# A decoder block on one core: more block products in the MLP, weight sums of the down projection formed in DRAM, another order of the background work

## The chip, the cores and the metric

The kernel runs on one core of one Trainium2 chip. The metric is device time of one execution in microseconds (us), lower is better. Engines are named as in the profile: PE is TensorE's matmul, PEld its weight load, DVE is VectorE, ACT ScalarE, POOL GpSimd, SP SyncE; "SPq" and "POOLq" in a row are the issuing of a DMA on that engine's queue.

## The reference

One layer on 512 rows of width 1024, all in float32: a sparse attention with three branches, a sliding-window attention, an MLP with a causal convolution of width 3, and a gated side input. What matters here is the MLP:

```python
h = x @ w_in            # and both attentions: queries, keys, gates, ...
x = x + rmsnorm(concat(o_nsa, o_swa) @ w_o, attn_post_g)
h = rmsnorm(x, mlp_pre_g)
a, u = split(h @ w_gate_up, [2816])           # 1024 -> 2 x 2816
a = causal_dwconv(a, conv_w, conv_b)
y = (gelu(a, approximate=True) * u) @ w_down  # 2816 -> 1024
x = x + rmsnorm(y, mlp_post_g)
x = x + (p @ w_ple) * sigmoid(x @ w_ple_gate)
```

## The kernel before

**Products.** Each float32 operand is held as two float32r parts, a high part and the remainder. `mm3` forms a product by three matmuls into one PSUM bank: high by high (L165), low by high (L168), high by low (L169). A weight of 128 x 1024 arrives raw by one DMA on SyncE (`raw`, L154; or L156); ACT copies its high part (L144) and DVE subtracts it to get the low part (L148), both in `weight`. There are three pairs of slots for split weights ("wh"), two for raw ones ("wr"), and others among tags such as "p" and "kn".

**Up stage (`mlp_up`).** The 2816 columns make 22 tiles of 128 columns, each with a gate weight and an up weight; tiles 0 and 1 are done first, from weights that were ready earlier. A plain tile is two gemms of 8 products on 512 columns: 48 matmuls of 512 columns. Up to tile `RAW_LAST` the gemms take the rows before their normalization and the result is scaled by the row factors afterwards: DVE L1161, POOL L1163 in `mlp_tile`. Later tiles take normalized rows (`hn`), which `normalized` makes in small steps between the gemms, with their half sums (`ht`, L1052 to L1062). After that each tile ends in the convolution and the gelu (`conv`, DVE L1146, ACT L1144 and L1147) and is kept as two parts in `y`.

**Blocked tiles.** The tiles in `BLOCKED` use a scheme of seven half-size products in place of eight (`blocked_tile`): 84 matmuls of 256 columns. It needs sums of parts of the weights. These are formed in DRAM: a DMA on SyncE copies a part (`block_copies`, 256 KB each, 28 of them, issued in attention, one at every third call of `fill` after the tenth), then DMAs with addition on POOL's queue add other parts to it (`block_additions`, L1199, 28 of them), three after each gemm of the up stage. `fill` is called between the steps of attention to put filling matmuls, loads and copies there; its DMA is `load_late` (L295). Moves of the queries and keys to the partitions where attention wants them are `move` (L298), also on SyncE.

**Down stage (`mlp_down`).** Eight output tiles of 128 columns; six go as three pairs (`pair_of_tiles`), of whose 22 input tiles the first twelve are done as six block products and the others plainly. For a block product a weight of 256 KB is loaded and DVE forms the three sums with four operations on 128 columns (`block_weight`, L1079 to L1082) before ACT and DVE split it. The half sums of `y` are made by `sums_of` (L1068 and `half_sums`). Each pair uses six PSUM banks, and `block_sums` puts them together.

**What sets the order.** The program text gives each engine its instructions through a scheduler that keeps the order where it is told to (`keep_in_program_order`), and moves the rest. `pin` ties a DMA with addition behind a given matmul. A DMA on SyncE waits on its own queue for the slot that it fills and for the sum that it reads; what stands behind it on SyncE waits too.

Of the kernel before, what the change touches and what calls it, by code (L numbers as in the profile page):

```python
# [76 lines left out]
COPY_FROM, COPY_STEP = 10, 3


class Block:  # L80
# [971 lines left out]
    def half_sums(self, b, t, parts):  # L1052
# [5 lines left out]
        nc.vector.tensor_sub(t[:, 3, :], b[1][0], t[:, 1, :])  # L1058
        for i, o in enumerate(parts):
            v = t[:, 2 * i : 2 * i + 2, :].rearrange("p a n -> p (a n)")  # L1060
            nc.scalar.activation(o[:, 0, :], v, AF.Copy)
            nc.vector.tensor_sub(o[:, 1, :], v, o[:, 0, :].bitcast(F32))  # L1062

    def sums_of(self, i):
# [5 lines left out]
        self.half_sums([[f[:, k, hs] for hs in HALF] for k in range(2)], self.u([P, 4, H], F32, STAG[i]), self.tt[i])  # L1070

    def block_weight(self, c, i, tag):

# [1 line left out]
        r = self.wrp.tile([P, 7 * P], F32, tag="wr", name=self.nm("wr")) if tag == "wr" else self.u([P, 7 * P], F32, tag)
        src = self.io["down"][c : c + 2, :, 2 * i * P : (2 * i + 2) * P].rearrange("c p n -> p c n")
        nc.sync.dma_start(r[:, : 4 * P].rearrange("p (c n) -> p c n", c=2), src)
        b = [r[:, k * P : (k + 1) * P] for k in range(7)]
        nc.vector.tensor_sub(b[4], b[0], b[2])  # L1079
        nc.vector.tensor_add(b[2], b[2], b[3])  # L1080
        nc.vector.tensor_sub(b[5], b[2], b[0])
        nc.vector.tensor_sub(b[6], b[1], b[5])  # L1082
        return self.weight(r, 7 * P, early=True)

    def block_products(self, c, i, wt, banks, last=False):
        d, e, p1, p5, p6, p7 = banks
        y1, y2 = self.y[2 * i], self.y[2 * i + 1]
        ta, tb = self.tt[i]
        a, b = slice(0, H), slice(H, T)
        for ps, k, x in ((p1, 0, y1[:, :, a]), (p6, 5, ta[:, :, b]), (p7, 4, tb[:, :, a]), (p5, 2, ta[:, :, a])):  # L1090
            self.mm3(ps[:, a], wt, k * P, x, i == 0, i == KP - 1)
        for ps, k, x in ((d[:, a], 1, y2[:, :, a]), (d[:, b], 6, y2[:, :, b]), (e[:, a], 3, tb[:, :, b])):
            self.mm3(ps, wt, k * P, x, False, last and k != 1)
# [398 lines left out]
```

## Time and profile before

| | |
|---|---|
| median of 3 runs | 666.39 us (665.5 to 667.02) |
| the profiled execution | 662.78 us |
| its span in the profile | 660.9 us |
| granted TensorE clock | 1.00 |
| up stage, by PE | 252.4 to 489.3 us |
| down stage, by PE | 489.3 to 611.3 us |
| busy: PE, DVE, ACT, POOL | 646.9, 501.9, 361.2, 174.3 us |

Attention lies before 223.3 us, the output projection and the norm between 223.3 and 252.4, the last norm and the gated side input after 611.3. In a row of the timeline the first two numbers are the start and the length in us, then come engine, line, operation, output <- inputs by the program's names; in square brackets stands how long the engine had been idle and what ended it. In a row of the waits the three numbers are the total in us, how often, and the longest. In a row of a window: the stretch, its length, the busy time of PE, PEld, DVE, ACT and POOL with the count of instructions, the granted clock, the DMA engines' busy share and GB/s. In a row of DMA issues the last two numbers are the size of one transfer and the median time from issue to landing in us.

### The profile page before, as it was taken

Reading aid. Unit: us, or ns where it says so; the run is one execution under the profiler, and the core shown is the slowest. Engines: PE = TensorE matmul, PEld = TensorE weight load, DVE = VectorE, ACT = ScalarE, POOL = GpSimd, SP = SyncE. Lnnn points to the kernel's source line nnn. Section 1 sums busy time; section 2 is a strip of 40 time slices with the busy share of each in tenths; the row PEclk is TensorE's granted clock in tenths of the full one; section 3 lists DMA queues with packets and bytes.
Section 4 is the critical chain, followed back from the end, with each engine's and each line's share of the span. In section 5 each row is a group of like instructions: output and inputs, shape, how many; then the busy total and the mean of one; then the engine's idle time right before and its main releaser. Section 6 shows DMA issues by size and latency. Waiting matters only on the chain.

```text
span 660.9 us, 10545 instructions
## 1 busy us (share of the span) xinstructions
PE 646.9 (98%) x3701; PEld 563.3 (85%) x3701; DVE 501.9 (76%) x1048; ACT 361.2 (55%) x667; POOL 174.3 (26%) x260
## 2 busy tenths in 40 slices
PE   9999899999999999999999999999999999999997
PEld 8988678878888888888778889998898898899986
DVE  6895587978756469699998766767699876757873
ACT  7464487978888476445465544554444434334351
POOL 1111488678487163216330000000000010102000
PEclk9999999999999999999999999999999999999999
DMA  8437891321364529929774355343322234287032
GB/s 302 170 108 242 272 339 42 83 55 50 80 187 164 160 95 257 300 81 182 170 229 154 121 165 160 123 131 113 96 75 87 72 113 127 66 293 258 31 112 79
DMA packets 39076, 98.22 MB, mean 149 GB/s; under 512 B 4656, under 2 KB 12848, under 8 KB 37680
## 3 DMA queue, kind: packets, MB, share of 16 engines
q1 hardware_dynamic: 37536, 90.13, 41.7%
q0 software_dynamic: 1344, 7.34, 6.2%
q8 instruction: 29, 0.48, 0.3%
q14 instruction: 23, 0.19, 0.1%
q10 hardware_dynamic: 144, 0.08, 0.1%
HBM read 83.90 MB, written 20.97 MB: 159 GB/s over the span
## 4 chain that ended last, share of the span: by engine, by line
PE 73%; DVE 15%; DMA 5%; ACT 3%; issue 2%; POOL 0%; SPq 0%; ACTq 0%; DVEq 0%
DMA mlpdown_wr<-in_down_dram 3%; PE mlpup_pss L168 3%; PE mlpup_pss L169 3%; PE mlpup_pss L165 3%; DVE mlpdown_wh L148 2%; PE nsa_pso L613 2%; DVE mlpup_s L1146 2%; PE nsa_pst L580 2%; PE mlpup_psmm L168 2%; PE mlpup_psmm L169 2%; PE mlpup_psmm L165 2%; PE mlpup_pst L169 2%; PE mlpup_pst L168 2%; PE mlpup_pst L165 2%; DVE mlpup_wh L148 2%
## 5 line engine op out<-in xcount | busy, mean ns | idle before, releaser
L291 POOL TENSOR_TENSOR mlpdown_s<-mlpdown_s,mlpdown_s 128x512 f32<-128x512 f32 x6 | 8.9, 1478 | 241.3 <-ACT mlpdown_s L290 241.2
L144 ACT ACTIVATE mlpup_wh<-mlpup_wr 128x1024 fp32r<-128x1024 f32 x31 | 32.7, 1056 | 32.8 <-DMA mlpup_wr<-in_gu_dram 8.5
L144 ACT ACTIVATE mlpdown_wh<-mlpdown_wr 128x896 fp32r<-128x896 f32 (+2 forms) x27 | 26.3, 979 | 43.0 <-DMA mlpdown_wr<-in_down_dram 15.5
L148 DVE TENSOR_TENSOR mlpup_wh<-mlpup_wr,mlpup_wh 128x1024 fp32r<-128x1024 f32 x31 | 37.8, 1219 | 9.9 <-PE mlpup_psmm L168 4.7
L603 POOL TENSOR_SCALAR nsa_u<-nsa_u,nsa_nrc,gate 128x512 f32<-128x512 f32 (+3 forms) x64 | 38.6, 615 | 15.0 <-DVE nsa_nrc L739 9.9
L705 ACT ACTIVATE nsa_u<-nsa_u,nsa_nnm 128x512 f32<-128x512 f32 (+3 forms) x64 | 35.4, 554 | 7.2 <-DVE nsa_nnm L698 7.1
L148 DVE TENSOR_TENSOR mlpdown_wh<-mlpdown_wr,mlpdown_wh 128x896 fp32r<-128x896 f32 (+2 forms) x27 | 31.2, 1163 | 9.3 <-ACT mlpdown_wh L144 8.8
L165 PE MATMUL mlpup_pss<-mlpup_u,mlpup_wh 128*128 128x256 f32 (+1 forms) x108 | 34.8, 322 | 0.1
L168 PE MATMUL mlpup_pss<-mlpup_u,mlpup_wh 128*128 128x256 f32 (+1 forms) x108 | 34.8, 322 | 0.0
L169 PE MATMUL mlpup_pss<-mlpup_u,mlpup_wh 128*128 128x256 f32 (+1 forms) x108 | 34.8, 322 | 0.0
L585 DVE TENSOR_TENSOR nsa_u<-nsa_pst,nsa_u 128x512 fp32r<-128x512 f32 (+1 forms) x43 | 29.4, 686 | 6.8 <-ACT nsa_u L582 6.5
L1146 DVE SCALAR_TENSOR_TENSOR mlpup_s<-mlpup_s,cols,mlpup_s 128x511 f32<-128x511 f32 (+1 forms) x30 | 27.3, 913 | 6.2 <-ACT mlpup_s L1144 6.0
L148 POOL TENSOR_TENSOR fill_wh<-fill_wr,fill_wh 128x1024 fp32r<-128x1024 f32 (+2 forms) x13 | 24.5, 1887 | 28.7 <-ACT fill_wh L144 28.7
L698 DVE CUSTOM_DVE_ANT_0 nsa_u<-nsa_pss,biastables_u 128x224 f32<-128x224 f32 (+3 forms) x64 | 27.9, 447 | 5.4 <-PE nsa_pss L639 4.8
L148 DVE TENSOR_TENSOR mlpup_wh<-mlpup_u,mlpup_wh 128x1024 fp32r<-128x1024 f32 x16 | 19.6, 1224 | 14.2 <-ACT mlpup_wh L144 11.2
L582 ACT ACTIVATE nsa_u<-nsa_pst 128x512 fp32r<-128x512 f32 x43 | 25.4, 593 | 8.5 <-PE nsa_pst L580 8.1
L144 ACT ACTIVATE mlpup_wh<-mlpup_u 128x1024 fp32r<-128x1024 f32 x16 | 17.0, 1060 | 22.1 <-PE mlpup_pss L168 11.2
L168 PE MATMUL mlpup_psmm<-mlpup_u,mlpup_wh 128*128 128x256 f32 (+1 forms) x88 | 27.5, 313 | 1.3 <-DVE mlpup_wh L148 1.3
L169 PE MATMUL mlpup_psmm<-mlpup_u,mlpup_wh 128*128 128x256 f32 (+1 forms) x88 | 27.4, 312 | 0.0
L165 PE MATMUL mlpup_psmm<-mlpup_u,mlpup_wh 128*128 128x256 f32 (+1 forms) x88 | 27.4, 311 | 0.0
L613 PE MATMUL nsa_pso<-nsa_u,vnatural_u 128*128 128x512 f32 x72 | 25.8, 423 | 0.4 <-DVE nsa_s L597 0.2
L165 PE MATMUL mlpdown_psmm<-mlpup_u,mlpdown_wh 128*128 128x512 f32 (+1 forms) x76 | 26.0, 344 | 0.0
(535 smaller groups left out, 2372.9 us busy)
## 6 DMA issues: line engine op xcount, KB each, us to landing
mlpup_wr<-in_gu_dram SPq DMA_DIRECT2D x17, 512.0 KB, 3.9
blocks<-in_gs_dram SPq DMA_DIRECT2D x28, 256.0 KB, 5.5
mlpup_u<-in_gu_dram SPq DMA_DIRECT2D x9, 512.0 KB, 4.1
blocks<-in_gs_dram POOLq DMA_DIRECT2D x14, 256.0 KB, 7.2
blocks<-blocks POOLq DMA_DIRECT2D x14, 256.0 KB, 5.0
mlpup_wr<-in_gs_dram SPq DMA_DIRECT2D x7, 512.0 KB, 3.5
mlpup_wr<-blocks SPq DMA_DIRECT2D x7, 512.0 KB, 4.0
mlpup_u<-blocks SPq DMA_DIRECT2D x7, 512.0 KB, 3.7
```

The source lines that it names most:

```text
L144: h = nc.scalar.activation(hi, raw, AF.Copy)
L148: l = eng.tensor_sub(lw, raw, hi.bitcast(F32))
L165: r = self.pin(mm(ps, hi, x[:, 0, :], start=start, stop=False))
L168: mm(ps, lo, x[:, 0, :], start=False, stop=False)
L169: self.last = mm(ps, hi, x[:, 1, :], start=False, stop=stop).ins
L582: nc.scalar.activation(t[:, 0, :], pt, AF.Copy)
L585: nc.vector.tensor_sub(t[rs, part, :], pt[rs], t[rs, 0, :].bitcast(F32))
L603: self.nc.gpsimd.tensor_scalar(ap, ap, col, gate, op0=ALU.mult, op1=ALU.mult)
L613: self.att(nc.tensor.matmul(po, v, t[:, part, :], start=start, stop=stop))
L698: nc.vector.tensor_tensor_reduce(dst, src, dist, op0=ALU.add, op1=ALU.min, scale=SLOPES[8 + 4 * g + r], scalar=start, accum_out=out)
L705: nc.scalar.activation(dst, dst, AF.Exp, bias=nm[:, r, b : b + 1], scale=-1.0, accum_out=sm[:, r, b : b + 1])
L1146: nc.vector.scalar_tensor_tensor(c[:, k:], a[:, : T - k], w(2 - k), c[:, k:], op0=ALU.mult, op1=ALU.add)
```

## The change

- **Blocked tiles.** Eight, tiles 10, 11, 13, 14, 16, 17, 19 and 20, instead of seven (9, 11, 13, 15, 17, 19, 21). `RAW_LAST` goes from 7 to 6.
- **Down.** The host packs the parts of the down weights of the three pairs (`gd`), and their sums are formed in DRAM (`down_sums`) by the same copies and additions as in up, 384 KB each: 12 copies and 12 additions. Two blocks go together as a group with two weights (1024 and 768 columns), each raw weight by two DMAs (L1083 now), and DVE forms no sums of weights any more. A pair uses four PSUM banks instead of six. `ORDER` says where the groups stand among the plain parts.
- **Copies.** 32 of 256 KB in attention, from call 44 on at every fourth; the 12 of 384 KB are issued in the up stage, one after each gemm from the fifth on.
- **Additions.** One after each gemm up to tile 9, then two; a blocked tile first issues all that its pair of tiles in `BLOCKED` needs.
- **Normalized rows.** All eight normalized tiles first, one step after each gemm; the half sums begin when tile 6's `y` is there, in eight steps, two after each gemm.

```diff
-ORDER = [[range(0, 3), (), range(3, 6)], [range(0, 3), range(3, 6), ()], [range(6), (), ()]]
+ORDER = [[(0,), (), (1, 2)], [(0,), (1, 2), ()], [(0, 1, 2), (), ()]]
-BLOCKED = [9, 11, 13, 15, 17, 19, 21]
+BLOCKED = [10, 11, 13, 14, 16, 17, 19, 20]
-RAW_LAST = 7
+RAW_LAST = 6
-COPY_FROM, COPY_STEP = 10, 3
+COPY_FROM, COPY_STEP = 44, 4
...
-        for c in self.copies:
-            c()
...
+    def group_weights(self, c, g):
+        nc = self.nc
+        gd, d = self.io["gd"][c // 2], self.down_sums[c // 2]
+        for srcs in ((gd[0:2, g], d[2:4, g]), (d[0:2, g], gd[3:4, g])):
+            tag, n = next(self.rawtag), sum(x.shape[0] for x in srcs) * 2 * P
+            t = self.wrp.tile([P, n], F32, tag="wr", name=self.nm("wr")) if tag == "wr" else self.u([P, n], F32, tag)
+            at = 0
+            for x in srcs:
+                w = x.shape[0] * 2 * P
+                nc.sync.dma_start(t[:, at : at + w].rearrange("p (s n) -> p s n", n=2 * P), x.rearrange("s p n -> p s n"))
+                at += w
+            yield self.weight(t, n, early=True)
+
+    def group_products(self, c, g, banks, last):
+        d, e, f, o = banks
+        a, b = HALF
+        for k, wt in enumerate(self.group_weights(c, g)):
+            for i in (2 * g, 2 * g + 1):
+                y1, y2 = self.y[2 * i], self.y[2 * i + 1]
+                ta, tb = self.tt[i]
+                if k == 0:
+                    todo = ((o[:, a], y1[:, :, a], i == 0), (d[:, a], y2[:, :, a], False),
+                            (f[:, b], tb[:, :, a], i == 0), (o[:, b], ta[:, :, a], False))
+                else:
+                    todo = ((f[:, a], ta[:, :, b], False), (d[:, b], y2[:, :, b], False), (e[:, a], tb[:, :, b], False))
...
-        banks = [self.ps(k) for k in (t, t, "s", "s", "s", "o")]
+        banks = [self.ps(k) for k in (t, t, "s", ("s", "o", "s")[c // 2])]
...
+    def normalized(self, x1):
+        nc = self.nc
+        fs = []
+        for k in range(KC):
...
+            self.hn.append(h)
             yield
+        while len(self.y) <= RAW_LAST:
+            yield
+        for kp, f in enumerate(fs):
+            parts = [self.u([P, 2, T], F32R, PTAG[2 * kp + i]) for i in range(2)]
+            self.ht += parts
+            yield from self.half_sums([[f[:, i, hs] for hs in HALF] for i in range(2)], self.u([P, 4, H]), parts)
...
+        self.down_sums = [self.dp.tile([4, 3, P, 2 * P], F32, name=f"downblocks{i}") for i in range(MP)]
+        pairs = [(d, self.io["gs"][i]) for i, d in enumerate(self.sums_in)]
+        pairs += [(d.rearrange("s g p n -> s (g p) n"), self.io["gd"][i].rearrange("s g p n -> s (g p) n"))
+                  for i, d in enumerate(self.down_sums)]
...
+        def background(n):
+            self.pinned = self.last
+            for _, a in zip(range(n), adds):
+                a()
+                added[0] += 1
+            self.pinned = None
+
         for j in range(NB // 2, NFF):
             if j in BLOCKED:
+                for _ in todo:
+                    pass
+                background(8 * (BLOCKED.index(j) // 2 + 1) - added[0])
                 self.blocked_tile(j, [next(cyc) for _ in range(4)])
...
                     n += 1
-                    self.pinned = self.last
-                    for _ in range(3):
-                        next(adds, lambda: None)()
-                    self.pinned = None
+                    if n > 4:
+                        next(self.copies, lambda: None)()
+                    background(1 if j < BLOCKED[0] else 2)
                     if n > 1:
-                        for _ in range(2):
+                        for _ in range(1 if j <= RAW_LAST else 2):
                             next(todo, None)
                 self.mlp_tile(j, pp[0], pp[1])
+
+        background(4 * len(self.scratch) - added[0])
```

SyncE's queue in attention, between the query moves of one part (`projq_u`) and the moves of the keys (`compress_u`); `blocks` are the copies, `fill_wr` weight loads. Before:

```order
L156 DMA fill_wr_846<-in_win_dram 128x1024
L295 DMA blocks_975<-in_gs_dram 16x4096 x3
L298 DMA projq_u_701<-projq_u_698 64x512 x4
L295 DMA blocks_975<-in_gs_dram 16x4096
L295 DMA blocks_976<-in_gs_dram 16x4096
L156 DMA fill_wr_1159<-in_win_dram 128x1024
L295 DMA blocks_976<-in_gs_dram 16x4096 x2
L298 DMA compress_u_455<-projk_u_768 64x512 x2
```

The same place with the change:

```order
L156 DMA fill_wr_846<-in_win_dram 128x1024
L298 DMA projq_u_701<-projq_u_698 64x512 x4
L156 DMA fill_wr_1146<-in_win_dram 128x1024
L295 DMA blocks_1349<-in_gs_dram 16x4096 x2
L298 DMA compress_u_455<-projk_u_768 64x512 x2
```

Seven copies stood there ahead of the key moves, three of them ahead of the query moves; two stand there now.

DVE in the up stage, between two splits of weights (L148) where half sums and tile ends lie close. Before, twelve operations between the two:

```order
L148 TENSOR_TENSOR mlpup_wh_3908<-mlpup_wr_3905,mlpup_wh_3907 128x1024
L1062 TENSOR_TENSOR mlpup_u_3631<-mlpup_u_3630,mlpup_u_3631 128x512
L1146 SCALAR_TENSOR_TENSOR mlpup_s_3819<-mlpup_s_3820,cols,mlpup_s_3819 128x511
L1056 TENSOR_TENSOR mlpup_u_3696<-mlpup_u_3641,mlpup_u_3696 128x256
L1161 TENSOR_TENSOR mlpup_s_3894<-mlpup_pst_3837,r3b 128x512
L1166 TENSOR_TENSOR mlpup_s_3741<-mlpup_psmm_3713,mlpup_s_3741 128x512
L1062 TENSOR_TENSOR mlpup_u_3632<-mlpup_u_3630,mlpup_u_3632 128x512
L1146 SCALAR_TENSOR_TENSOR mlpup_s_3819<-mlpup_s_3820,cols,mlpup_s_3819 128x510
```

With the change the fullest stretch between two splits has seventeen operations, eight of them on 256 columns (its first twelve rows):

```order
L148 TENSOR_TENSOR mlpup_wh_3980<-mlpup_wr_3977,mlpup_wh_3979 128x1024
L1172 TENSOR_TENSOR mlpup_s_3871<-mlpup_pst_3833,mlpup_s_3871 128x512
L1053 TENSOR_TENSOR mlpup_u_3915<-mlpup_u_3597 128x256
L1055 TENSOR_TENSOR mlpup_u_3915<-mlpup_u_3597 128x256
L1053 TENSOR_TENSOR mlpup_u_3959<-mlpup_u_3684 128x256
L1055 TENSOR_TENSOR mlpup_u_3959<-mlpup_u_3684 128x256
L1054 TENSOR_TENSOR mlpup_u_3915<-mlpup_u_3597,mlpup_u_3915 128x256
L1159 TENSOR_TENSOR mlpup_u_3877<-mlpup_s_3871,mlpup_u_3877 128x512
L1054 TENSOR_TENSOR mlpup_u_3959<-mlpup_u_3684,mlpup_u_3959 128x256
L1056 TENSOR_TENSOR mlpup_u_3915<-mlpup_u_3597,mlpup_u_3915 128x256
L1152 SCALAR_TENSOR_TENSOR mlpup_s_3968<-mlpup_pss_3886,cols,mlpup_s_3968 128x511
L1056 TENSOR_TENSOR mlpup_u_3959<-mlpup_u_3684,mlpup_u_3959 128x256
```

This stretch lies between the splits of tile 9's two weights; between the splits of tiles 4 to 8, and up to the first of tile 9, there are three to nine operations.

DVE in the down stage, over a change of pair. Before:

```order
L148 TENSOR_TENSOR mlpdown_wh_5720<-mlpdown_u_5713,mlpdown_wh_5719 128x896
L1079 TENSOR_TENSOR mlpdown_wr_5794<-mlpdown_wr_5794 128x128
L148 TENSOR_TENSOR mlpdown_wh_5767<-mlpdown_wr_5764,mlpdown_wh_5766 128x1024
L1080 TENSOR_TENSOR mlpdown_wr_5794<-mlpdown_wr_5794 128x128
L1079 TENSOR_TENSOR mlpdown_u_5825<-mlpdown_u_5825 128x128
L1081 TENSOR_TENSOR mlpdown_wr_5794<-mlpdown_wr_5794 128x128
L1080 TENSOR_TENSOR mlpdown_u_5825<-mlpdown_u_5825 128x128
L1102 TENSOR_TENSOR mlpdown_s_5744<-mlpdown_u_5299,mlpdown_pss_5436 128x256
```

With the change:

```order
L148 TENSOR_TENSOR mlpdown_wh_5762<-mlpdown_wr_5758,mlpdown_wh_5761 128x1024
L148 TENSOR_TENSOR mlpdown_wh_5793<-mlpdown_u_5789,mlpdown_wh_5792 128x768
L148 TENSOR_TENSOR mlpdown_wh_5836<-mlpdown_wr_5833,mlpdown_wh_5835 128x1024
L148 TENSOR_TENSOR mlpdown_wh_5867<-mlpdown_wr_5863,mlpdown_wh_5866 128x1024
L1110 TENSOR_TENSOR mlpdown_s_5814<-mlpdown_u_5389,mlpdown_pss_5524 128x256
```

The splits of the next pair now follow each other with nothing between, and the putting together of the last pair (L1110) comes behind them.

More of the change, by code (lines that the diff above doesn't have):

```diff
@@ L1069, in sums_of @@
         self.tt.append([self.u([P, 2, T], F32R, t) for t in TTAG[2 * i : 2 * i + 2]])
-        self.half_sums([[f[:, k, hs] for hs in HALF] for k in range(2)], self.u([P, 4, H], F32, STAG[i]), self.tt[i])
-    def block_weight(self, c, i, tag):
+        for _ in self.half_sums([[f[:, k, hs] for hs in HALF] for k in range(2)], self.u([P, 4, H], F32, STAG[i]), self.tt[i]):
+            pass
+    def group_weights(self, c, g):
         nc = self.nc
[L1075 to L1093, printed above, removed]
+        gd, d = self.io["gd"][c // 2], self.down_sums[c // 2]
@@ new lines, in group_products @@
+    def group_products(self, c, g, banks, last):
[10 more added lines that the diff above has]
+                    todo = ((f[:, a], ta[:, :, b], False), (d[:, b], y2[:, :, b], False), (e[:, a], tb[:, :, b], False))
+                for n, (ps, x, start) in enumerate(todo):
+                    own = (k, n) not in ((0, 1), (1, 1), (1, 2))
+                    self.mm3(ps, wt, (2 * n + i % 2) * P, x, start, i == KP - 1 and (own or last and k == 1), shared=own)
@@ L1130, in pair_of_tiles @@
                     self.sums_of(i)
-            blocks(ks)
+            for g in ks:
+                self.group_products(c, g, banks, more)
             if c == 2 * MP - 2 and len(ks):
@@ L1192, in block_copies @@
+        flat = lambda t: t.rearrange("s p n -> s (p n)").rearrange("s (q e) -> q s e", e=ROWS)
+        self.scratch = [(flat(d), flat(g)) for d, g in pairs]
+        for d, g in self.scratch:
             for k in range(4):
-                yield lambda i=i, d=d, k=k: self.load_late(rows(d[k]), rows(self.io["gs"][i, k]))
+                self.copied += 1
+                yield lambda d=d, g=g, k=k: self.load_late(d[:, k], g[:, k])
     def block_additions(self):
-        nc, gs = self.nc, self.io["gs"]
@@ new lines, in block_additions @@
+        add = lambda o, a: self.pin(nc.gpsimd.dma_start(o, a, accum_op=ALU.add, max_dma_last_dim=4 * ROWS))
+        for lo in range(0, len(self.scratch), 2):
+            some = self.scratch[lo : lo + 2]
+            while self.copied < 4 * min(lo + 2, len(self.scratch)):
+                next(self.copies)()
+            for d, g in some:
+                yield lambda d=d, g=g: add(d[:, 2], g[:, 0])
+                yield lambda d=d, g=g: add(d[:, 3], g[:, 2])
+            for d, g in some:
+                yield lambda d=d: add(d[:, 0], d[:, 3])
+            for d, g in some:
+                yield lambda d=d: add(d[:, 1], d[:, 0])
@@ L1289, in mlp_up @@
         adds = self.block_additions()
-        todo = itertools.chain(*(self.normalized(x1, kp) for kp in range(KC // 2)))
+        todo = self.normalized(x1)
+        added = [0]
+        def background(n):
[4 more added lines that the diff above has]
+            self.pinned = None
         for j in range(NB // 2, NFF):
             if j in BLOCKED:
+                for _ in todo:
+                    pass
+                background(8 * (BLOCKED.index(j) // 2 + 1) - added[0])
                 self.blocked_tile(j, [next(cyc) for _ in range(4)])
@@ L1296, in mlp_up @@
                 for i in range(2):
-                    wt = ahead.pop(0) if ahead else self.weight(self.raw(io["gu"][2 * j + i], tag=next(self.rawtag) if j > RAW_LAST else "wr"), early=True)
+                    wt = ahead.pop(0) if ahead else self.weight(self.raw(io["gu"][2 * j + i], tag=next(self.rawtag) if j >= BLOCKED[0] - 1 else "wr"), early=True)
                     ps = self.ps(next(cyc))
```

63 lines of the change are left out of this document (24 added, 39 removed).

## The prediction

> **What bounds the kernel now.** I read the head of the page first, then the busy time by stage (the up stage, the down stage, a crowded stretch, one plain and one blocked tile of the up stage), then TensorE's waits.
>
> ```profile
> span 660.9 us, 10545 instructions
> PE 646.9 (98%) x3701; PEld 563.3 (85%) x3701; DVE 501.9 (76%) x1048; ACT 361.2 (55%) x667; POOL 174.3 (26%) x260
> ...
> 252.40:489.30 236.90, 233.98 (x1301) 204.43 (x1301) 193.24 (x258) 119.40 (x162) 32.72 (x32) 1.00 0.55 158
> 489.30:611.30 122.00, 120.02 (x776) 109.36 (x775) 94.82 (x186) 46.76 (x63) 9.59 (x7) 1.00 0.45 143
> 300.00:350.00 50.00, 47.08 (x207) 38.13 (x206) 50.00 (x73) 27.40 (x40) 21.84 (x21) 1.00 0.77 190
> 385.76:396.69 10.93, 10.93 (x51) 9.02 (x49) 8.09 (x11) 4.36 (x7) 0.00 (x0) 1.00 0.40 123
> 396.69:406.71 10.02, 10.02 (x86) 10.02 (x84) 6.50 (x8) 5.71 (x7) 0.00 (x0) 1.00 0.49 156
> ```
>
> TensorE (PE) is busy for 98% of the span at a granted clock of 1.00, so 660.9 - 646.9 = 14.0 us is all that removing waits can give, and less matmul work is the only other source. In the row of 300 to 350 PE idles 2.9 us of 50 while DVE is busy for all 50: there DVE is the limit. Which waits they are:
>
> ```profile
> PE mlpdown_pss L168 <- DVE mlpdown_wh L148: 1.8, 2, 1.1
> PE nsa_pss L638 <- DMA compress_u<-projk_u: 1.6, 1, 1.6
> ...
> PE mlpup_pst L165 <- ACT mlpup_wh L144: 1.5, 1, 1.5
> PE mlpup_psmm L168 <- DVE mlpup_wh L148: 1.3, 1, 1.3
> PE nsa_pss L639 <- DMA compress_u<-projk_u: 0.3, 1, 0.3
> ```
>
> These five lines, 6.5 us together, lie where the change works: weights split too late in down (1.8) and up (1.5 + 1.3), keys moved too late in attention (1.6 + 0.3).
>
> **Attention: -1.7 us.** SyncE's queue ahead of the late keys, and two pieces of the chain there, the last of which ends the wait:
>
> ```profile
> 59.58 1.82 SPq L295 DMA_DIRECT2D blocks<-in_gs_dram  x3
> 61.50 3.88 SPq L298 DMA_DIRECT2D projq_u<-projq_u  x4
> 65.42 1.22 SPq L295 DMA_DIRECT2D blocks<-in_gs_dram  x2
> ...
> 67.32 1.12 SPq L295 DMA_DIRECT2D blocks<-in_gs_dram  x2
> 68.54 6.40 SPq L298 DMA_DIRECT2D compress_u<-projk_u  x8
> ...
> 70.98 0.30 DVE nsa_u L698
> ...
> 71.51 3.41 DMA compress_u<-projk_u
> ```
>
> Between the query moves and the eight key moves stand seven copies, 1.82 + 1.22 + 1.12 = 4.16 us of issuing, besides the bytes they put ahead. Copies now start at call 44 instead of 10, and two remain in this place: five copies fewer, 5 x 0.6 = 3.0 us earlier, against a wait of 1.6 + 0.3 = 1.9. I take 1.7, since the chain's DVE piece before it ends only at 71.3. Bounds: 0 (another input is late by as much) to -1.9.
>
> The other 30 copies for the up stage, four more in all, follow later in attention, one at every fourth call instead of every third; the moves there stand on no row of PE's waits, and I cost these copies at nothing. The 12 new copies of 384 KB go out in the up stage, one after each weight from tile 4 on. What the engines do there, from the stretches 59 to 90 (copies) and 262 to 280 (spills and additions):
>
> ```profile
> DMA packets 2531, 9.19 MB, mean 296 GB/s; under 512 B 652, under 2 KB 652, under 8 KB 2212
> ...
> mlpup_wr<-in_gu_dram SPq DMA_DIRECT2D x2, 512.0 KB, 9.1
> ```
>
> At 296 GB/s a copy of 0.393 MB takes 1.3 us. Under a plain tile that makes two copies, 2.7; its loads, 0.40 x 10.93 = 4.4; two additions, 3.1 (below): 10.2 of 10.93 us. It fits, so nothing; but were loads to land as late as the 9.1 row, 9.1 + ACT 1.06 + DVE 1.22 = 11.4 against a slot that comes back after two weights, 10.93, and twelve weights cost 12 x 0.23 = 2.7. Bounds 0 and +2.7.
>
> **Up stage, order of the normalized tiles: -2.8 us, and +1.3 back.** The rows around its two stalls:
>
> ```profile
> 329.94 1.06 ACT L144 ACTIVATE mlpup_wh<-mlpup_wr 128x1024 fp32r<-128x1024 f32 x1 [4.65 <-DMA mlpup_wr<-in_gu_dram]
> ...
> 337.90 0.42 DVE L1058 TENSOR_TENSOR mlpup_u<-mlpup_u,mlpup_u 128x256 f32<-128x256 f32 x1
> 338.23 1.22 DVE L148 TENSOR_TENSOR mlpup_wh<-mlpup_wr,mlpup_wh 128x1024 fp32r<-128x1024 f32 x1
> 339.37 0.69 DVE L1062 TENSOR_TENSOR mlpup_u<-mlpup_u,mlpup_u 128x512 fp32r<-128x512 f32 x1
> 339.97 1.78 DVE L1146 SCALAR_TENSOR_TENSOR mlpup_s<-mlpup_s,cols,mlpup_s 128x511 f32<-128x511 f32 x1
> ...
> 343.81 0.74 DVE L1146 SCALAR_TENSOR_TENSOR mlpup_s<-mlpup_s,cols,mlpup_s 128x510 f32<-128x510 f32 x1
> ...
> 348.38 1.22 DVE L148 TENSOR_TENSOR mlpup_wh<-mlpup_u,mlpup_wh 128x1024 fp32r<-128x1024 f32 x1
> ```
>
> From one weight's low part to the next DVE took 348.38 - 338.23 = 10.15 us, twelve operations; a plain weight lasts PE 10.93 / 2 = 5.47. Some operations are slower beside a POOL multiplication (1.78 against 0.74). The change spreads the eight normalized tiles first, one step to a weight, and starts the sixteen half sums only when tile 6's output exists, two yields to a weight up to tile 10. The same DVE work has one more plain tile to lie under, 10.93 us, and is thin until tile 6, so that three weights can stand ready when the thick part comes. One thick gap is left in the new order, seventeen operations between two low parts: eight of 256 columns, two convolution steps, seven others of 512, or 8 x 0.42 + 2 x 0.74 + 7 x 0.69 = 9.7, with the split 1.22 it is 10.9 us. That equals the lead of two weights (2 x 5.47), so it is covered if both really are ahead; I charge one repeat of the present stall, +1.3. Bounds: 0 if the lead is full, and +2.8 if the DVE limit merely moves to tiles 7 to 9.
>
> **One more blocked tile: -0.9 us.** 10.93 - 10.02 = 0.91, from the two windows; the count of matmuls in down is unchanged. The last tile is plain now and the half sums of x are dead one tile earlier; that only helps.
>
> **Down stage: -1.8 us.** What leaves it, and what its loads take:
>
> ```profile
> L1082 DVE TENSOR_TENSOR mlpdown_wr<-mlpdown_wr x12: 279/291/295, 506.5 to 579.6; 128x128 f32<-128x128 f32 x12
>   ACT mlpdown_wh L144: 8.6, 6
> ...
> 515.41 0.38 PE L168 MATMUL mlpdown_pss<-mlpup_u,mlpdown_wh 128*128 128x256 f32 x1 [1.06 <-DVE mlpdown_wh L148]
> ...
> mlpdown_wr<-in_down_dram SPq DMA_DIRECT2D x5, 512.0 KB, 3.9
> mlpdown_u<-kept_x SPq DMA_DIRECT2D x4, 512.0 KB, 6.1
> ```
>
> 72 operations on 128 columns (four to each of 18 weights), 72 x 0.29 = 20.9 us of DVE in 122, disappear; ACT waited 8.6 us for the last of each four before it could start on a weight, and both PE stalls of the list's first row are behind such weights. They go: -1.8, bounds 0 to -1.8. The new weights are as wide on average, 896 columns, but come ready-made, 448 KB instead of 256, in two transfers. A load of 512 KB lands in 3.9; with ACT 1.06 and DVE 1.22 that is 6.2 us, against three raw slots in turn, each back after three weights: a weight feeds 21 matmuls of 256 columns on average, at 10.02 / 84 = 0.12 us each 2.5, so 7.5 us. Hidden, then; if they landed like the 6.1 row the cover would be gone: 8.4 - 7.5 is 0.3 to a weight, 18 x 0.3 = 5.4 us.
>
> **Additions and loads beside the blocked tiles.** Sixteen additions more, and 34 of the 44 now come after tile 6's multiplication:
>
> ```profile
> 345.35 1.30 POOL L1163 TENSOR_TENSOR mlpup_s<-mlpup_s,r3b 128x512 f32<-128x512 f32 x1 [4.15 <-ACT mlpup_s L1147]
> 296.09 0.79 POOL L1199 DMA_DIRECT2D blocks<-blocks  x1
> ...
> 294.84 2.51 DVE mlpup_s L1146 x2
> ...
> q0 software_dynamic: 721, 3.93, 57.3%
> ...
> mlpup_wr<-in_gu_dram SPq DMA_DIRECT2D x5, 512.0 KB, 4.6
> blocks<-blocks POOLq DMA_DIRECT2D x9, 256.0 KB, 4.8
> blocks<-in_gs_dram POOLq DMA_DIRECT2D x6, 256.0 KB, 6.3
> ```
>
> The last four rows are of the stretch 300 to 340: fifteen additions in 40 us, 2.7 each, of which 0.573 x 2.7 = 1.55 is time of all DMA engines. 22 of 256 KB and 12 half again as large, from 345 on, end at 345 + 22 x 2.7 + 12 x 4.0 = 453 us; down reads the first new sums at about 495. Hidden, 42 us ahead. Loads of 512 KB landed in 4.6 beside them, and a blocked tile's four loads have 10.02 us for a slot's 4.6 + 2.3. I cost this at nothing.
>
> [...]
>
> **Sum.** -1.7 - 2.8 + 1.3 - 0.9 - 1.8 = -5.9. The profiled execution took 662.78, so 656.9; the median, 666.39, lies 3.6 above that execution, and against it the forecast is **660.5 us**.
>
> **Rivals.** *The up stall stays.* DVE's full 50 us speak for it, the thinner order up to tile 6 against: both stalls return, 660.5 - 1.3 + 2.8 = 662.0. *The keys are late for another reason.* For it: DVE's piece that ends at 71.3; against, 3.41 us of nothing but that transfer: 660.5 + 1.7 = 662.2. *Given back in adjoining blocked tiles.* Three times two blocked tiles now follow each other, without a plain tile's 5.47 us to a weight to rebuild the lead; if each time one split, ACT 1.06 + DVE 1.22, is bare: 660.5 - 1.3 + 3 x 2.28 = 666.0, no change. *Slower: loads late under the additions.* Additions now run under tiles 10 to 17, not only under plain ones. A blocked tile wants 0.49 of the DMA engines; the additions' 0.573 leave 0.427, and the tile would take 10.02 x 0.49 / 0.427 = 11.5, 1.5 more; six tiles, 8.9, to 669.4. It decides where a 512 KB load lands later than 10.02 - 2.28 = 7.7 us. The 4.6 speaks against. *Slower: the sums late for down.* Were each addition to wait for the one before to land, 4.8 instead of 2.7, the ninth of the larger ones, the last for the first pair, would end at 345 + 22 x 4.8 + 9 x 7.2 = 515, 20 after need: 681.
>
> **How the numbers follow.** Forecast 0.50, with its own range 658.5 to 662.5 (all new costs nothing, or each at its near bound); up stall 0.18; keys 0.08; adjoining tiles 0.09; loads late 0.12; sums late 0.03. 0.2%, 1.3 us, is about what can be told from no change. Faster 0.50 + 0.18 + 0.08 = 0.76, same 0.09, slower 0.15. The range, 656.5 to 669, takes in the four gains in full (-7.2: 659.2), the runs' spread of 1.5 us and 1.2 of the idle time that I have not named, and ends inside the load case.
>
> **What would show it.** Right: no wait on the key moves near 72 us; none on a split weight in the up stage beyond one of about 1.3; none at the head of a block group in down; 512 KB loads under the blocked tiles landing below 7.7; the last addition landed before 490. Wrong: DVE full over 40 us after tile 6 with PE waiting, a PE wait in the second of two adjoining blocked tiles, or a SyncE load standing on a late sum.

## The result, and the profile after

| | before | changed |
|---|---|---|
| median | 665.94 us (665.08 to 667.02, 4 runs) | 671.05 us (669.82 to 672.41, 4 runs) |
| profiled execution | 662.78 us | 672.41 us |
| span | 660.9 us | 670.7 us |
| up stage, by PE | 252.4 to 489.3 us | 254.7 to 502.4 us |
| down stage, by PE | 489.3 to 611.3 us | 502.4 to 620.6 us |

The ratio is 1.0076, with a 95% interval of 1.0049 to 1.0103: the change is slower by 5.1 us. The forecast was 660.5 and its range ended at 669.

The page's head, TensorE's waits and four stretches of the changed kernel (110 us with the normalized tiles and half sums; 66 us from the first blocked tile on; 6 us inside these; the down stage):

```profile
span 670.7 us, 10629 instructions
PE 650.0 (97%) x3737; PEld 567.3 (85%) x3737; DVE 481.7 (72%) x985; ACT 362.9 (54%) x670; POOL 182.8 (27%) x275
...
PE mlpup_pss L165 <- ACT mlpup_wh L144: 3.7, 1, 3.7
PE mlpup_pss L168 <- DVE mlpup_wh L148: 3.7, 3, 2.1
PE mlpup_pst L168 <- DVE mlpup_wh L148: 2.1, 3, 1.0
...
PE nsa_pss L639 <- DMA compress_u<-projk_u: 0.8, 1, 0.8
...
PE nsa_pss L638 <- DMA compress_u<-projk_u: 0.6, 1, 0.6
...
254.00:364.00 110.00, 110.00 (x487) 90.84 (x486) 97.18 (x132) 56.75 (x81) 24.10 (x24) 1.00 0.70 205
364.00:430.00 66.00, 56.41 (x389) 52.26 (x388) 37.81 (x52) 26.55 (x36) 18.14 (x23) 0.95 0.99 263
420.00:426.00 6.00, 4.85 (x21) 4.56 (x22) 2.42 (x3) 1.55 (x4) 0.78 (x1) 0.50 1.02 296
502.40:620.60 118.20, 117.95 (x764) 107.76 (x763) 73.55 (x113) 48.27 (x64) 9.41 (x7) 1.00 0.53 173
```

Both old waits of the up stage are gone: PE is busy for all 110 us up to the first blocked tile, where before it waited 1.5 and 1.3. The waits at the block groups in down are gone too. What came in their place stands in one stretch: from 364 to 430 us PE idles 9.6 of 66 us, and the three rows of waits on split weights make 9.5 of it. Of these, 6.3 us lie in the blocked tiles 10, 11 and 14, the other 3.1 in the plain tiles 12 and 15, which follow a pair of blocked ones. In the 6 us from 420 on PE works at a granted clock of 0.50. There the DMA engines are full (0.99). They are nearly as full from 340 to 364 us already (0.98), and PE does not wait there yet; the first wait comes at 367.

Who fills them, from the DMA answer for the same 66 us of the changed kernel, and the chain of waits over the longest of them:

```profile
q0 software_dynamic: 1346, 7.87, 59.1%
q1 hardware_dynamic: 4411, 9.41, 39.7%
...
mlpup_u<-blocks SPq DMA_DIRECT2D x4, 512.0 KB, 9.8
mlpup_wr<-blocks SPq DMA_DIRECT2D x3, 512.0 KB, 8.7
...
mlpup_wr<-in_gu_dram SPq DMA_DIRECT2D x2, 512.0 KB, 14.2
```

```profile
402.89 1.24 DVE mlpup_wh L148
404.13 0.02 issue
404.15 15.11 DMA mlpup_wr<-blocks
...
419.36 1.06 ACT mlpup_wh L144
420.43 0.02 issue
420.45 1.24 DVE mlpup_wh L148
```

The load of 512 KB is issued at once when its slot comes free (404.15), not held by a sum that is late; it takes 15.11 us to land, where loads of that size took 3.5 to 4.3 (medians) in the kernel before between 385 and 448 us:

```profile
mlpup_wr<-in_gs_dram SPq DMA_DIRECT2D x3, 512.0 KB, 3.5
...
mlpup_wr<-blocks SPq DMA_DIRECT2D x3, 512.0 KB, 4.3
```

59.1% of the engines' time goes to the DMAs with addition (q0), nearly all of the rest to loads (q1). POOL's timeline, with the first and the last of the additions behind tile 6's multiplication:

```profile
337.36 2.19 POOL L1169 TENSOR_TENSOR mlpup_s<-mlpup_s,r3b 128x512 f32<-128x512 f32 x1 [4.42 <-ACT mlpup_s L1153]
339.50 1.60 POOL L1214 DMA_DIRECT2D blocks<-in_gs_dram  x2
...
422.29 0.78 POOL L1214 DMA_DIRECT2D downblocks<-downblocks  x1 [4.14 <-DMA downblocks<-downblocks]
```

The program puts them one or two behind each gemm, but that only orders them. With no multiplication of tiles left to wait for, POOL issues all 34 from 339.5 to 422.3 us; of the 56.8 us that it idles between them, 52.6 end with the landing of a DMA of these sums.

By stages of PE: the work up to the up stage is 2.3 us longer (254.7 against 252.4), nearly all of it in the sliding-window attention (67.0 to 69.5); the up stage's matmuls take 247.7 instead of 238.1 from start to start, +9.6; down's take 2.4 less (the 1.3 us of the last up tile that reached behind down's first matmul before are counted with up). 2.3 + 9.6 - 2.4 = 9.5, against 672.41 - 662.78 = 9.6.

### The profile page after: what moved, and what is told of

Its sections match the earlier page's. It is cut to its first block, busy times and chain, and to the rows that moved or that the text cites. A ratio compares the mean times of both kernels' runs of the same rounds, so it can differ in the third digit from the quotient of the medians.

```text
span 670.7 us, 10629 instructions
## 1 busy us (share of the span) xinstructions
PE 650.0 (97%) x3737; PEld 567.3 (85%) x3737; DVE 481.7 (72%) x985; ACT 362.9 (54%) x670; POOL 182.8 (27%) x275
## 4 chain that ended last, share of the span: by engine, by line
PE 60%; DVE 15%; DMA 12%; ACT 5%; issue 3%; SPq 2%; POOL 2%; ACTq 0%; DVEq 0%; POOLq 0%
DVE mlpup_wh L148 3%; DMA mlpup_wr<-blocks 2%; DVE mlpup_s L1152 2%; PE nsa_pst L580 2%; DMA mlpup_u<-blocks 2%; PE mlpdown_psmm L165 2%; PE nsa_pso L613 2%; PE mlpdown_psmm L168 2%; PE mlpdown_psmm L169 2%; DMA mlpup_wr<-in_gu_dram 2%; PE mlpup_pss L168 2%; PE mlpup_pss L169 2%; PE mlpup_pss L165 2%; PE mlpdown_pst L165 1%; PE mlpdown_pst L169 1%
## 5 line engine op out<-in xcount | busy, mean ns | idle before, releaser
L144 ACT ACTIVATE mlpup_wh<-mlpup_wr 128x1024 fp32r<-128x1024 f32 x33 | 34.7, 1052 | 46.3 <-DMA mlpup_wr<-blocks 25.0
L148 DVE TENSOR_TENSOR mlpup_wh<-mlpup_wr,mlpup_wh 128x1024 fp32r<-128x1024 f32 x33 | 41.1, 1244 | 21.6 <-ACT mlpup_wh L144 21.5
L148 DVE TENSOR_TENSOR mlpdown_wh<-mlpdown_wr,mlpdown_wh 128x1024 fp32r<-128x1024 f32 (+1 forms) x27 | 31.7, 1174 | 34.4 <-ACT mlpdown_wh L144 34.4
L144 ACT ACTIVATE mlpdown_wh<-mlpdown_wr 128x1024 fp32r<-128x1024 f32 (+1 forms) x27 | 26.7, 989 | 51.9 <-PE mlpdown_psmm L168 11.5
L168 PE MATMUL mlpup_pss<-mlpup_u,mlpup_wh 128*128 128x256 f32 (+1 forms) x112 | 36.9, 330 | 3.7 <-DVE mlpup_wh L148 3.7
L165 PE MATMUL mlpup_pss<-mlpup_u,mlpup_wh 128*128 128x256 f32 (+1 forms) x112 | 36.7, 328 | 3.8 <-ACT mlpup_wh L144 3.7
L169 PE MATMUL mlpup_pss<-mlpup_u,mlpup_wh 128*128 128x256 f32 (+1 forms) x112 | 36.4, 325 | 0.0
L1152 DVE SCALAR_TENSOR_TENSOR mlpup_s<-mlpup_s,cols,mlpup_s 128x511 f32<-128x511 f32 (+1 forms) x30 | 24.4, 815 | 11.8 <-ACT mlpup_s L1150 11.6
L148 POOL TENSOR_TENSOR fill_wh<-fill_wr,fill_wh 128x1024 fp32r<-128x1024 f32 (+2 forms) x13 | 24.5, 1884 | 29.5 <-ACT fill_wh L144 21.2
L168 PE MATMUL mlpup_psmm<-mlpup_u,mlpup_wh 128*128 128x256 f32 (+1 forms) x96 | 30.9, 322 | 0.0
L169 PE MATMUL mlpup_psmm<-mlpup_u,mlpup_wh 128*128 128x256 f32 (+1 forms) x96 | 30.9, 322 | 0.0
L165 PE MATMUL mlpup_psmm<-mlpup_u,mlpup_wh 128*128 128x256 f32 (+1 forms) x96 | 30.8, 323 | 0.0
L168 PE MATMUL mlpup_pst<-mlpup_u,mlpup_wh 128*128 128x256 f32 (+1 forms) x88 | 28.6, 325 | 2.1 <-DVE mlpup_wh L148 2.1
L1169 POOL TENSOR_TENSOR mlpup_s<-mlpup_s,r3b 128x512 f32<-128x512 f32 x7 | 11.0, 1570 | 70.1 <-ACT mlpup_s L1153 70.1
L165 PE MATMUL mlpup_pst<-mlpup_u,mlpup_wh 128*128 128x256 f32 (+1 forms) x88 | 28.4, 322 | 0.1
L169 PE MATMUL mlpup_pst<-mlpup_u,mlpup_wh 128*128 128x256 f32 (+1 forms) x88 | 28.1, 321 | 0.0
```

Of the source, the lines that this page charges most:

```text
L144: h = nc.scalar.activation(hi, raw, AF.Copy)
L148: l = eng.tensor_sub(lw, raw, hi.bitcast(F32))
L165: r = self.pin(mm(ps, hi, x[:, 0, :], start=start, stop=False))
L168: mm(ps, lo, x[:, 0, :], start=False, stop=False)
L169: self.last = mm(ps, hi, x[:, 1, :], start=False, stop=stop).ins
L1152: nc.vector.scalar_tensor_tensor(c[:, k:], a[:, : T - k], w(2 - k), c[:, k:], op0=ALU.mult, op1=ALU.add)
```

## The experiments

The theory after the result: crowding. The additions, run in one burst, share the DMA engines with the weight loads of the blocked tiles; the loads land too late. Its rivals: two adjoining blocked tiles have too little lead however the additions lie; the DMA demand is too much however it is spread. Each kernel is compared with runs of the kernel before on the same chip; the first four with 665.75 us, the next four with 664.62, the last three with 664.65. Kernels of different groups ran on different chips.

### The additions held to the pace of PE

```diff
-            self.tc.add_manual_dep(r.ins, self.pinned.name, mybir.DependencyInfo(
-                mybir.DependencyClass.NoSync, mybir.DependencyReason.DATA), reason="filler")
+            kind = mybir.DependencyClass.Sync if self.paced else mybir.DependencyClass.NoSync
+            self.tc.add_manual_dep(r.ins, self.pinned.name, mybir.DependencyInfo(
+                kind, mybir.DependencyReason.DATA), reason="filler")
...
-                    background(1 if j < BLOCKED[0] else 2)
+                    background(1)
...  blocked_tile, after the products of a weight
+            if len(products) > 1:
+                self.background(1)
```

> The changed kernel, with each DMA with addition held until the gemm or block weight before it has run on PE (a real wait), one after each gemm and one after each of the first three weights of a blocked tile. Theory (crowding): in the changed kernel POOL ran the additions as fast as it could, 34 of them between 339 and 429 us, the DMA engines were full there, loads of 512 KB landed after 7 to 19 us and the blocked tiles waited for 9.5 us, with the clock at 0.50 for a further 2 to 3. Spread out, the loads land in under 8 us and the waits go: 671.05 - 11 = 660, between 658 and 663. Rival (adjoining blocked tiles have too little lead by themselves): the waits stay in the second tile of each pair, 669 to 671. Rival (the DMA demand is too much however it is spread): waits spread out to tile 20, 666 to 669.

Measured: 657.02 us (656.62 to 659.25), 0.9897 of before, 0.9871 to 0.9924. This beats both kernels. Two stretches of this kernel, then lines of the DMA answer for the second:

```profile
254.00:364.00 110.00, 110.00 (x492) 91.25 (x491) 99.00 (x134) 58.63 (x83) 23.35 (x23) 1.00 0.69 206
364.00:430.00 66.00, 66.00 (x468) 62.16 (x468) 49.62 (x67) 34.60 (x47) 13.31 (x18) 1.00 0.82 219
```

```profile
q0 software_dynamic: 816, 4.46, 38.3%
...
mlpup_wr<-blocks SPq DMA_DIRECT2D x5, 512.0 KB, 4.9
mlpup_u<-blocks SPq DMA_DIRECT2D x5, 512.0 KB, 6.2
```

PE is busy for all 66 us at clock 1.00, through the same adjoining blocked tiles. The same 44 additions now end at 480 us instead of 429, and the loads of these two rows land after about 5 to 6 us. Both rivals fall. One wait on a split weight is left in the up stage, 0.6 us at 445, in the plain tile behind the third pair.

### Two additions after every gemm, without a wait

```diff
-                    background(1 if j < BLOCKED[0] else 2)
+                    background(2)
```

> The changed kernel with two additions after every gemm from the start of the up stage, instead of one up to tile 9 and two later; nothing else. Crowding: the 32 additions for up are done by about tile 9, under plain tiles whose weights last 5.5 us, and only the 12 for down fall under blocked tiles; the waits of 9.5 us fall to about 4, time 662 to 666, with 0 to 3 us of new waits in tiles 4 to 9. Adjoining blocked tiles: 669 to 671, no change.

Measured: 663.99 us (659.74 to 665.39, 10 runs), 0.9976 of before, 0.9953 to 0.9999. Waits on weights in the up stage are 4.0 us (2.4 + 1.1 + 0.5); the additions end at 407 us. As crowding says.

### Without the additions for down

```diff
-        background(4 * len(self.scratch) - added[0])
...
-            for _, a in zip(range(n), adds):
+            for _, a in zip(range(min(n, 4 * len(BLOCKED) - added[0])), adds):
```

> The changed kernel without the 12 additions that form the weight sums for down; the copies stay, and down multiplies with unfinished sums, the same count of matmuls. Crowding: the waits after 392 us (3.7 + 1.1 + 1.2 us, and about 2 at the clock of 0.50) go, those at 367 to 390 (about 4.5) stay: 671 - 8 = 663. Adjoining blocked tiles: 669 to 671.

Measured: 662.99 us (661.91 to 664.3, 10 runs), 0.9969 of before, 0.9954 to 0.9983. Waits of 2.1, 0.9, 0.7 and 0.2 us are left in the up stage, all before 389. The twelve larger additions were worth the expected 8 us.

### The copies in attention early again

```diff
-COPY_FROM, COPY_STEP = 44, 4
+COPY_FROM, COPY_STEP = 10, 3
```

> The changed kernel with the copies in attention from call 10 on at every third call, as before the change. If the later copies cost the 2.5 us that the sliding-window attention became longer (from 67.0 to 69.5 us): keys wait 1.9 again (+0.5), window attention back at 67, time 669. If that was the order of instructions and not the copies: window attention stays at 69.5 and the time is 671.5.

Measured: 672.48 us (668.28 to 674.81), 1.0116 of before, 1.0073 to 1.016. The waits of this kernel in attention:

```profile
PE nsa_pss L638 <- DMA compress_u<-projk_u: 2.8, 1, 2.8
PE swa_pss L638 <- DMA fill_u<-fill_u: 1.1, 1, 1.1
PE swa_pss L638 <- DVE swa_nm L660: 0.5, 1, 0.5
```

The keys wait 2.8 + 0.2 = 3.0 us, against 1.4 in the changed kernel. One pair of profiles says little here, since this wait varies: in the six kernels with the early copies (this one, the kernel before and the four built on it below) it is 1.9 to 3.3 us, in the six with copies from call 44 on it is 0 to 1.5, on average 1.8 less. So starting the copies late does help there. But the window attention stays long (69.9 us). Its lengthening is not from where the copies start.

### The same places, without the wait

The paced kernel, with the additions ordered as before the pacing and not held:

```diff
-            self.pinned, self.paced = self.last, True
+            self.pinned, self.paced = self.last, False
```

> The additions at the same places of the program as in the paced kernel (one after each gemm, one after each of the first three weights of a blocked tile), but without the wait for PE, so that POOL may issue them as soon as it reaches them. If it is the wait that spreads them: POOL runs ahead as in the changed kernel, the additions end near 430 us, loads land late, 669 to 672. If the places alone are enough: 657 to 659.

Measured: 662.9 us (661.19 to 665.08, 10 runs), 0.997 of before, 0.9951 to 0.9988. Neither number was met. The stretch of the blocked tiles in this kernel:

```profile
364.00:430.00 66.00, 61.55 (x411) 56.40 (x411) 46.61 (x64) 31.15 (x42) 17.38 (x22) 0.97 1.00 267
```

The DMA engines are full (1.00), the additions end at 433 us, and PE idles 4.4 us there. So POOL did run ahead, as the first theory says: from the same places the additions end at 433 us without the wait for PE and at 480 with it. The waits up to 390 us are alike in both (4.3 us here, 4.0 in the changed kernel); the later ones, 5.4 there, are missing here. Why was not tried.

### Without any addition

```diff
             for _, a in zip(range(n), adds):
-                a()
                 added[0] += 1
```

> The changed kernel without any of the 44 additions; the copies stay, the block products use unfinished sums, the count of matmuls is the same. Crowding: without them no wait is left in the blocked tiles, 656 to 658, about the time of the paced kernel (657.0). If the paced additions still cost something on PE: a few us below 657. Adjoining blocked tiles with too little lead: waits at the second tiles of the pairs stay, above 660.

Measured: 656.67 us (654.75 to 657.05), 0.9869 of before, 0.984 to 0.9899. The same stretches of this kernel:

```profile
254.00:364.00 110.00, 110.00 (x489) 91.12 (x489) 99.03 (x134) 58.65 (x83) 11.06 (x7) 1.00 0.48 171
364.00:430.00 66.00, 66.00 (x468) 62.16 (x467) 50.05 (x68) 35.16 (x47) 0.00 (x0) 1.00 0.48 154
```

No wait is left in these stretches. The paced kernel, measured on another chip, stood at 0.9897 of before (0.9871 to 0.9924); the intervals overlap. Held to PE's pace, 44 additions cost nothing that is clear of the noise: the ratios differ by 0.0028, 1.9 us.

### The kernel before with the new order of normalized rows

The new `normalized`, the two yields in `half_sums` and the last raw tile 6, in the kernel before:

```diff
-RAW_LAST = 7
+RAW_LAST = 6
...
-        todo = itertools.chain(*(self.normalized(x1, kp) for kp in range(KC // 2)))
+        todo = self.normalized(x1)
...
-                        for _ in range(2):
+                        for _ in range(1 if j <= RAW_LAST else 2):
                             next(todo, None)
```

> The kernel before with one part of the change: the normalized tiles first, one step to a gemm, then the half sums, two steps to a gemm, and the last raw tile 6; blocked tiles, copies, additions and down as before. If the order alone takes the two waits of 1.5 and 1.3 us away: 665.75 - 2.8 = 663. If the half sums, now under tiles 7 and 8 alone, fill DVE there: waits of 1 to 4 us at the first blocked tile, 665 to 668.

Measured: 671.12 us (668.96 to 672.6), 1.009 of before, 1.0055 to 1.0124. A miss: slower. The two low parts of weights at the ends of one stretch of DVE, the stretch itself, and PE's wait there:

```profile
337.94 1.22 DVE L148 TENSOR_TENSOR mlpup_wh<-mlpup_wr,mlpup_wh 128x1024 fp32r<-128x1024 f32 x1
...
355.80 1.21 DVE L148 TENSOR_TENSOR mlpup_wh<-mlpup_u,mlpup_wh 128x1024 fp32r<-128x1024 f32 x1
...
337.94:355.80 17.86, 10.92 (x47) 8.50 (x45) 16.52 (x34) 9.51 (x16) 2.18 (x1) 0.93 0.45 148
...
PE mlpup_psmm L165 <- ACT mlpup_wh L144: 6.9, 1, 6.9
```

Thirty-two operations lie between the two splits, all sixteen half sums among them: 17.9 us, more than three weights' time on PE (16.4).

### The same, with the first blocked tile at 10

```diff
-BLOCKED = [9, 11, 13, 15, 17, 19, 21]
+BLOCKED = [10, 11, 13, 15, 17, 19, 21]
```

> As the last one, with the first blocked tile at 10 instead of 9 (10, 11, 13, 15, 17, 19, 21), so that the half sums lie under three plain tiles as in the change; seven blocked tiles as before. If order and room together take both waits away: 663. If the pair 10, 11 has too little lead: a wait in tile 11, 664 to 666.

Measured: 671.44 us (670.16 to 673.22), 1.01 of before, 1.0063 to 1.0138, with the same wait (6.7). Another miss: room alone was not it. The 32 operations were still together.

### The same, with one more line of the change

```diff
-tag=next(self.rawtag) if j > RAW_LAST else "wr"
+tag=next(self.rawtag) if j >= BLOCKED[0] - 1 else "wr"
```

> As the kernel with the normalized tiles first and the first blocked tile at 10, with one more line of the change: raw weights go to the tag 'p' only from tile 9 on, not from tile 7. In the two runs before this one the scheduler put 32 operations between two splits of weights on DVE (17.9 us), and PE waited 6.7 to 6.9 us there; with this line the most is 17, as in the change. If that stretch was the whole cost: both old waits and the 6.9 go, 663 (662 to 664.5). If the order is costly in itself: 668 or more.

Measured: 661.78 us (659.24 to 663.74, 7 runs), 0.9949 of before, 0.9926 to 0.9973, and no wait of PE in the up stage. This line says from which tile on raw weights use slots of the tag "p"; with it the scheduler puts a split in the middle of the half sums, and the fullest stretch has the seventeen operations of the changed kernel. Order, room and this line together give the 2.9 us (664.65 - 661.78) that the forecast gave to the order; in the profiles the up stage takes 233.6 us from its first matmul to that of down, against 236.8 in the kernel before.

### More additions in the kernel before

```diff
         for j in range(NB // 2, NFF):
+            if j == 12:
+                self.pinned = self.last
+                for r in range(3):
+                    for d in self.sums_in[:2]:
+                        for k in range(4):
+                            flat = lambda t: t.rearrange("s p n -> s (p n)").rearrange("s (q e) -> q s e", e=ROWS)
+                            self.pin(nc.gpsimd.dma_start(flat(d[k : k + 1]), flat(io["gs"][0, k : k + 1]), accum_op=ALU.add, max_dma_last_dim=4 * ROWS))
+                self.pinned = None
```

> The kernel before with 24 more DMAs with addition of 256 KB, onto sums that have been read already, issued on POOL without a wait from tile 12 on; the output is untouched. Blocked tiles stand alone there (13, 15, 17). Crowding: the DMA engines fill for some 60 us, loads of 512 KB land after 8 us and more, PE waits 3 to 8 us in tiles 13 to 17, time 669 to 674. If only adjoining blocked tiles suffer: 665 to 666.5, no change.

Measured: 671.6 us (669.1 to 671.95), 1.0092 of before, 1.0067 to 1.0117. Two stretches of this kernel, lines of the DMA answer for 350 to 400 us, and two waits between 340 and 450:

```profile
364.00:400.00 36.00, 36.00 (x217) 32.16 (x216) 22.83 (x31) 15.34 (x21) 15.67 (x20) 1.00 0.93 224
409.70:412.70 3.00, 3.00 (x16) 3.00 (x16) 2.65 (x5) 1.75 (x2) 0.00 (x0) 0.50 0.70 206
...
q0 software_dynamic: 1010, 5.58, 57.0%
...
blocks<-in_gs_dram POOLq DMA_DIRECT2D x24, 256.0 KB, 11.5
...
mlpup_wr<-blocks SPq DMA_DIRECT2D x2, 512.0 KB, 12.9
...
PE mlpup_pss L165 <- ACT mlpup_wh L144: 3.6, 2, 3.0
...
PE mlpup_pss L168 <- DVE mlpup_wh L148: 0.9, 1, 0.9
```

With nothing of the change in it, a burst of additions makes loads land after up to 13 us and PE wait at a blocked tile that stands alone (3.0 and 0.9), again with a stretch at half clock behind. The additions began at 351.6 already, earlier than meant, since they waited for nothing either. Not all of the 7 us is theirs: the wait of 1.3 at about 349 in the kernel before is there too, 1.4 long, and here the clock stands at 0.72, 0.50 and 0.58 in 351 to 352, 352 to 354 and 354 to 355 us, where it is 1.00 in the kernel before: by the clock a loss of 1.7 us, an estimate.

### No copy ahead of the keys

The paced kernel with one more number changed:

```diff
-COPY_FROM, COPY_STEP = 44, 4
+COPY_FROM, COPY_STEP = 60, 4
```

> The paced kernel with the copies in attention from call 60 instead of 44, so that none stands ahead of the key moves. If the two copies there still held the keys up: the last wait there, 0.9 us, goes, 656. If the keys are late for another reason: 657.

Measured: 657.66 us (657.04 to 658.57), 0.9892 of before, 0.9873 to 0.991; no change beside the paced kernel. The wait on the keys is gone, and from the first key product to the window attention it takes 83.9 us instead of 85.5. But the kernel of "The same places, without the wait" still has the two copies ahead of its key moves, and its profile has no wait on the keys either and takes 84.2 us there. So this run does not show that the last two copies held the keys up. Elsewhere one wait on a split weight in the up stage grew from 0.6 to 1.7, and the window attention from 68.6 to 69.0.

## Why the prediction was wrong, point by point

- **The step that failed: additions and loads beside the blocked tiles, costed at nothing.** The end of the additions was hidden, as said: the 34 ran from 339.5 to 428.8 us, 89 us where 108 were forecast. The conclusion on the loads was wrong. "Loads of 512 KB landed in 4.6 beside them" came from a stretch under plain tiles, which take 0.40 of the DMA engines; the sum that stood in the rival, 0.573 and 0.49, is 1.06 under blocked tiles. There the loads of 512 KB landed after 7.7 to 14.2 us (medians), and PE waited 9.5 us and lost about 2.4 more at a clock of 0.50, an estimate from the clock. From its first matmul to that of down, the up stage takes 247.7 us, against 233.3 without any addition: the burst cost 14.4 us there. The kernel before had shown such a crowd, and the prediction used the 9.1 of this stretch only as a bound for the copies (262 to 280 us of the kernel before; additions, q0, and the other transfers, q1, together fill 104% of the engines' time by the profile's count):

```profile
q0 software_dynamic: 370, 2.06, 57.0%
q1 hardware_dynamic: 919, 3.36, 47.0%
...
mlpup_wr<-in_gu_dram SPq DMA_DIRECT2D x2, 512.0 KB, 9.1
```

- **The rival "slower: loads late under the additions" is what happened**, at 671.05 where it gave 669.4, by the point it named (a landing later than 7.7 us). It had a chance of 0.12, because the 4.6 us row was set against it; that row was of other tiles. That 669.4 lies so near is in part luck: it is 660.5 and a cost of 8.9, while the kernel without additions takes 656.67 and the burst cost 14.4. Nor are tiles stretched evenly, as the rival has it: single loads come late, a third of the waiting (3.1 of 9.5 us) falls in plain tiles, and the blocked tiles 16 and 17, after the burst, wait for nothing. The range ended inside this rival's case and should have held it whole. Whether the DMA engines themselves or the memory behind them set the limit, no run separates.
- **"Given back in adjoining blocked tiles"** is refuted, although the sign that was named for it came, a wait in the second tile of a pair (at 383 and 420 us): the kernel without additions has the same pairs and no wait in the up stage, the paced one only the 0.6, and the burst in the kernel before hurts a tile that stands alone.
- **Attention, -1.7.** The mechanism and its size hold on average: late copies shorten the wait on the keys by 1.8 us over the profiles of twelve kernels, though between the two profiles of the change it fell only from 1.9 to 1.4. Not foreseen: the window attention became longer by 1.6 to 2.9 us in the profiles of the kernels with the change, with the same matmuls (363) and new waits on DVE (`swa_nm` 0.5 to 1.2 us, `swa_s` up to 1.1). With the early copies it was no shorter. The scheduler's order there is the suspect; no run settled it.
- **Up stage, -2.8 and +1.3 back.** The -2.8 came (2.9 measured alone); the repeat of a stall that was charged did not: the stretch of seventeen operations was covered by the lead, as its own arithmetic said. But the reason given was incomplete: the order alone, and order and room together, cost 6.5 and 6.8 us; the raw slots' tag belongs to the mechanism, and the prediction had not listed that line.
- **One more blocked tile, -0.9.** Nothing speaks against it, but no run took it alone.
- **Down, -1.8.** Both waits went and the loads in two parts were hidden, as said; the size was 2.4, since from the start of one matmul to that of the next the two waits had cost that, not the 1.8 of idle time that the waits' row counts.
- **The issuing of the additions** was not what cost. The last ones were issued in 0.76 to 0.80 us each, in the changed kernel as before; what was late was the transfers (medians from issue to landing between 364 and 430 us: the additions for down 7.2 and 9.9 us, the loads of 512 KB 7.7 to 14.2).

Without the burst the total comes out near the forecast, but not term by term. The paced kernel, all of the change with real waits, has a span of 655.3 us against 660.9: -5.6, where the sum was -5.9. By stages that is +0.9 before the up stage (forecast -1.7), -3.9 in up (-2.4), -2.9 in down (-1.8) and +0.3 behind it. That the totals agree is luck: the longer window attention is made up for by larger gains in the MLP.

The medians differ by more, 657.02 against 665.75 or 8.7. The record lists a granted clock for 42 executions of the kernel before: the four at 1.00 took 662.7 to 663.2 us, the others, at 0.993 to 0.997, took 663.2 to 667.4. The profiled execution, 662.78 at 1.00, was thus one of the best, and the 3.6 us that the forecast added to reach the median go along with a lower clock. Three of the four runs of the paced kernel have 1.00. That it loses fewer stretches at half clock because it waits less is likely, but not shown.

## What to carry to other kernels

An order in the program is no pace: here POOL, with nothing of PE's to wait for, had issued its additions by 422 us, and held to PE's pace the last one landed at 480 instead of 429; a background transfer must wait for the work that it is meant to lie under. Before a background load is called hidden, add its share of the DMA engines to that of the stage where it will really run; at a sum of 1.06 the foreground loads paid here, with a first wait of PE at 367 us where the engines were full from 340 on, and a landing time measured under another stage misled (4.6 us, against 7.7 to 14.2). And a rule for the order of steps has to be read in the order that the scheduler makes of it: the same rule gave seventeen or thirty-two operations between two splits, by the tag of a buffer.

## What was not expected of the hardware

PE ran at half clock for a few us around the end of some waits, which made these dearer than they were long. The longest wait of the changed kernel, 3.7 us, ended at 420.5; the clock fell to 0.50 at about 419.4, near its end, and stayed there until 426.2. The matmuls of 256 columns start 0.21 us apart from 422.1 to 426.2 and 0.12 us apart from 426.5 on. PE was busy for 4.85 of the 6 us from 420 on, so by the clock half of that, about 2.4 us, was lost, an estimate. The length of a wait did not decide alone. The same wait of 2.12 us, at the same place, in the changed kernel and in the one without additions for down, each with a stretch behind it:

```profile
390.04 0.50 PE L168 MATMUL mlpup_pss<-mlpup_u,mlpup_wh 128*128 128x512 f32 x1 [2.12 <-DVE mlpup_wh L148]
...
390.00:392.00 2.00, 1.96 (x9) 1.64 (x10) 2.00 (x3) 1.26 (x2) 0.23 (x1) 1.00 0.95 219
```

```profile
388.05 0.69 PE L168 MATMUL mlpup_pss<-mlpup_u,mlpup_wh 128*128 128x512 f32 x1 [2.12 <-DVE mlpup_wh L148]
...
389.00:390.00 1.00, 1.00 (x4) 0.81 (x3) 1.00 (x1) 1.00 (x2) 0.21 (x1) 0.50 0.48 121
```

The first ran on at 1.00, the second at 0.50. What told these two waits apart, no run here shows.
